# Hybrid attention block on one core: attention written as three merged streams in a fixed TensorE order

## The chip, the cores and the metric

The kernel runs on one core of one Trainium2 chip. The time is the device time of one execution in microseconds (us). The core has five engines with instruction streams of their own: TensorE (PE in the profile, PEld for its weight loads), VectorE (DVE), ScalarE (ACT), GpSimd (POOL) and SyncE (SP), which here does nothing but issue DMA transfers. Each engine runs its own instructions in their order, and waits where an operand or a buffer isn't ready.

## The reference

One decoder block on x of shape (1, 1024, 1024) in float32:

```python
h = rms_norm(x, g_pre)
qa, ka, va, fa, za, qb, kb, vb, zb, gates = split(h @ w_in)
# branch a: 8 "fox" heads of 64, causal softmax attention with a forget term
logits = q @ k.T / 8 + c[:, None] - c[None, :]      # c = cumsum(log_sigmoid(fa + b_forget))
ya = softmax(causal(logits)) @ v * silu(za)
# branch b: 4 "diff" heads; q and k are pairs of 64, with rope
yb = (softmax(q1 @ k1.T) - lam * softmax(q2 @ k2.T)) @ v
yb = rms_norm(yb, g_subln) * (1 - lam_init) * silu(zb)
merged = sigmoid(gate_a) * (ya @ w_branch[0]) + sigmoid(gate_b) * (yb @ w_branch[1])
out = x + rms_norm(merged @ w_out, g_post)
```

## The kernel before

**Stages.** x is normalised and transposed into hT, and the v parts of the projection are computed and spilled to DRAM (0 to 111 us). Then come eight attention units (111 to 605): unit u = 0 to 3 is diff head u, unit 4 to 7 is a pair of fox heads. Then the gate projections g0 to g7 (605 to 775), in which each pair after g0 is computed by a Winograd-like scheme of seven products x1 to x7 of 12 matmuls (`gates_pair`, `wino`), the branch products pb (781 to 871) and the output (871 to 967).

**Precision.** Every product is made of three matmuls in a split format: an operand is cut into hi (a cast) and lo (the rest), and hi·hi, hi·lo and lo·hi are summed in PSUM. So a weight tile comes as a DMA into `raw_*`, a cast `hi_*` (POOL) and a subtraction `lo_*` (DVE); the probabilities P as a transposed tile `pt`, a cast `ph` (ACT) and a subtraction `pl` (DVE); and q and k as stacked tiles TA, TB (q) and KA, KB (k), which hold hi in one half of the partitions and lo in the other, with X0 and X1 as copies of TA and TB with the halves swapped, made by DMA (`swapped`). A logits piece `S` is two matmuls, one with TA and one with X0 (TB and X1 for the second map).

**A projection** (q, k or z of one unit) is two chunks of 512 columns, each 8 k-steps of 3 matmuls: `pk`, `pq`, `pz`. A q or k chunk is copied to `rawq`, `rawk` by ACT. For diff units its halves are swapped by four DMAs into `swq`, `swk`, multiplied by sines (POOL L292) and cosines (DVE L291), added (L293), and stacked (ACT L298 and L300, DVE L299 and L301). A z chunk goes to DRAM.

**A unit** has the groups g = 0 to 3 of two 128-row blocks (fox: for each of two heads). `row` computes the logits of one block in pieces of up to 512 columns into three PSUM buffers (`Sd`, `Sf`), from which DVE adds the bias and keeps the running extreme (L442, tile `mxd` or `mxf`); ACT takes the exponential (L446). In a diff unit POOL then combines the two maps (L534, L536). `av` transposes P (`ptd`, `ptf`), splits it, and multiplies with V (`ypd`, `ypf`). The order in the code is: the rows of a group, the products of the group behind (`pend`), then some tasks of a list `fill`, which holds the next unit's q and k chunks and z projections in whole chunks:

```python
tasks = [mk("k", 0, ...), mk("q", 0, ...), mk("k", 1, ...), mk("q", 1, ...)]
```

A scheduler with a time model of its own then sets the order of each engine's instructions, so that matmuls of a chunk, logits and products come out interleaved. The lists `ZFILL`, `TFILL` and `SFILL` say in which unit z projections, operand sums for the gates (`h_combinations`) and sums of squares for the diff heads' norm (`sum_squares`, ssq) stand.

**The gates.** For pair d two weights are fetched (`raw{d}_0`, `raw{d}_1`, L829). POOL forms sums S1 to S4 and splits the operands a2 and a4 (L685); ACT casts all seven. Between the pairs stand `y_work(t, c)`, which multiply the finished attention outputs (`yd` for t = 0 to 3, diff; `yf` for t = 4 to 7, fox) with norm factors `rb` and silu(z) `zs`: DVE, POOL (L797), ACT (L798), DVE. `YORD[d]` lists those that stand behind pair d. The branches then need `yT`, casts of yf and yd by ACT (L864), and weights `hi_br`.

## Time and profile before

| | us |
|---|---|
| three runs | 968.75, 968.38, 965.19 |
| median | 968.38 |
| the profiled execution | 969.32 |
| its span | 967.2 |
| mean granted PE clock | 0.982 |

The span is the time from the first to the last instruction that the profile shows. Rows of the timeline give start and duration in us, engine, line, operation, out<-in by the program's names without their numbers, and in brackets the idle time of that engine just before and what ended it. Matmuls are pipelined: one of 512 columns is shown with some 0.39 us, and the next starts 0.23 us after it. SPq rows are DMA issues; their duration is that of the issue, not of the transfer.

### The profile page before, as it was taken

What the parts mean: (1) busy time and instruction counts of PE and PEld (TensorE: products, weight loads), DVE (VectorE), ACT (ScalarE), POOL (GpSimd) and SP (SyncE); (2) the same over time, 40 slices, a digit from 0 to 9 for tenths busy, and PEclk for the clock granted to TensorE, in tenths of its full rate; (3) what the DMA queues carried; (4) which work ended last, traced back from release to release, by engine and by line L of the source; (5) the groups of instructions that cost most, each with busy time, mean ns of one, the idle gap of its engine ahead of it and who ended that gap; (6) DMA issues with size and microseconds to landing.
All of it is one profiled execution on the core that took longest, in us unless ns stands there. A gap on an engine that the chain in (4) does not pass through costs nothing. (4 is left out here: it accounts for less than half of the span.)

```text
span 967.2 us, 13623 instructions
## 1 busy us (share of the span) xinstructions
PE 902.9 (93%) x4608; PEld 752.5 (78%) x4608; DVE 614.8 (64%) x1100; ACT 416.0 (43%) x838; POOL 443.3 (46%) x401
## 2 busy tenths in 40 slices
PE   7999989999998999999999998999999879999993
PEld 5999867788777878878878887777887658887872
DVE  6731258878677657586585676147565683549866
ACT  3421124555555565475664767224333361313431
POOL 7100035546555364251331442236555636787964
PEclk9999989999999999999999999999999989999997
DMA  8532444425234353353443432984545696211232
GB/s 312 190 109 96 143 127 119 111 63 147 83 110 121 90 150 129 109 173 100 125 159 104 116 120 90 377 327 130 159 150 157 205 361 211 85 47 44 88 130 87
DMA packets 120710, 139.10 MB, mean 144 GB/s; under 512 B 11473, under 2 KB 85297, under 8 KB 119618
## 3 DMA queue, kind: packets, MB, share of 16 engines
q1 hardware_dynamic: 120642, 138.24, 44.8%
q8 instruction: 36, 0.59, 0.3%
q14 instruction: 32, 0.26, 0.1%
HBM read 87.76 MB, written 37.86 MB: 130 GB/s over the span
## 5 line engine op out<-in xcount | busy, mean ns | idle before, releaser
L198 PE MATMUL pv<-wvhi,hT 128*128 128x264 f32 (+2 forms) x384 | 89.0, 324 | 0.4 <-DVE hT L184 0.4
L733 PE MATMUL x_g<-T,a_g 128*128 128x512 f32 x336 | 80.9, 397 | 6.3 <-ACT a_g L684 5.5
L249 PE MATMUL pk<-hT,hi_k 128*128 128x512 f32 x256 | 85.1, 405 | 1.5 <-ACT rawk L286 1.5
L559 POOL TENSOR_TENSOR cb<-cb,trim 128x128 f32<-128x128 f32 x64 | 35.2, 552 | 111.3 <-DVE mxf L442 99.2
L875 PE MATMUL pb<-yT,hi_br 128*128 128x512 f32 x256 | 80.3, 397 | 5.8 <-ACT hi_br L235 5.8
L249 PE MATMUL pz<-hT,hi_z 128*128 128x512 f32 x256 | 83.6, 396 | 0.0
L249 PE MATMUL pq<-hT,hi_q 128*128 128x512 f32 x256 | 83.1, 396 | 0.0
L733 PE MATMUL x_o<-wo_op,a_o 128*128 128x512 f32 x336 | 77.9, 391 | 3.8 <-POOL a_o L685 2.5
L733 PEld LDWEIGHTS x_g<-T,a_g 128*128 128x128 f32 x336 | 63.8, 191 | 21.8 <-ACT a_g L684 6.8
L733 PEld LDWEIGHTS x_o<-wo_op,a_o 128*128 128x128 f32 x336 | 62.7, 188 | 18.8 <-POOL a_o L685 3.8
L446 ACT ACTIVATE Pd<-Pd,mxd 128x1024 f32<-128x1024 f32 (+7 forms) x64 | 49.7, 777 | 59.1 <-DVE mxd L442 58.7
L198 PEld LDWEIGHTS pv<-wvhi,hT 128*128 128x128 f32 x384 | 64.5, 190 | 6.1 <-DVE hT L184 0.7
L733 PE MATMUL x_g<-hT,a_g 128*128 128x512 f32 x252 | 61.4, 398 | 2.8 <-DVE a_g L685 2.8
L446 ACT ACTIVATE Pf<-Pf,mxf 128x768 f32<-128x768 f32 (+4 forms) x64 | 49.8, 778 | 29.3 <-DVE mxf L442 28.9
L198 PE MATMUL pv<-wvlo,hT 128*128 128x512 f32 (+2 forms) x192 | 61.8, 324 | 0.4 <-DVE wvlo L154 0.4
L471 DVE TENSOR_TENSOR plf<-ptf,phf 128x512 fp32r<-128x512 f32 (+1 forms) x80 | 50.1, 635 | 18.7 <-ACT phf L470 17.5
L875 PEld LDWEIGHTS pb<-yT,hi_br 128*128 128x128 f32 x256 | 49.1, 192 | 16.5 <-ACT hi_br L235 6.2
L733 PEld LDWEIGHTS x_g<-hT,a_g 128*128 128x128 f32 x252 | 48.3, 192 | 13.8 <-DVE a_g L685 3.7
L534 POOL TENSOR_SCALAR Pd<-Pd,l 128x128 f32<-128x128 f32 (+7 forms) x32 | 28.5, 893 | 65.7 <-DVE l L532 51.4
L249 PEld LDWEIGHTS pk<-hT,hi_k 128*128 128x128 f32 x256 | 48.1, 193 | 10.6 <-issue 1.9
L442 DVE CUSTOM_DVE_ANT_0 Pf<-Sf,cb 128x512 f32<-128x512 f32 (+1 forms) x64 | 36.1, 569 | 29.6 <-PE Sf L441 16.3
L249 PEld LDWEIGHTS pz<-hT,hi_z 128*128 128x128 f32 x256 | 47.4, 188 | 8.6
(250 smaller groups left out, 2352.8 us busy)
## 6 DMA issues: line engine op xcount, KB each, us to landing
t_d<-t SPq DMA_DIRECT2D x32, 256.0 KB, 2.5
T<-t_d SPq DMA_DIRECT2D x8, 1024.0 KB, 7.7
raw<-in_w_in_dram SPq DMA_DIRECT2D x14, 512.0 KB, 6.3
g_d<-c_g SPq DMA_DIRECT2D x21, 256.0 KB, 2.4
vb_d<-vbs SPq DMA_DIRECT2D x8, 512.0 KB
va_d<-vas SPq DMA_DIRECT2D x8, 512.0 KB, 3.6
raw_k<-in_w_in_dram SPq DMA_DIRECT2D x8, 512.0 KB, 5.3
raw_q<-in_w_in_dram SPq DMA_DIRECT2D x8, 512.0 KB, 4.0
```

The source lines that it names most:

```text
L198: nc.tensor.matmul(ps[n], lhsT=hT[hp][k // 4][i // 4][:, k % 4, hs], rhs=wt[k][:, a:b], start=first, stop=(k == KT - 1 and hp == 1))
L249: nc.tensor.matmul(ps, lhsT=a[:, k, :], rhs=hT[h][k // 4][c][:, k % 4, :], start=(k == 0 and a is hi and h == 0), stop=(k == KT - 1 and a ...
L442: nc.vector.tensor_tensor_reduce(out=pr[:, a:b], in0=ps, in1=bias[:, boff + a:boff + b], scale=-0.125, scalar=BIG if j == 0 else mx[:, j - ...
L446: nc.scalar.activation(pr[:, 0:n], pr[:, 0:n], AF.Exp, bias=mx[:, len(pcs) - 1:len(pcs)], scale=-1.0, accum_out=le)
L471: nc.vector.tensor_tensor(pl[:, 0:n], pt[:, 0:n], ph[:, 0:n], op=ALU.subtract)
L534: nc.gpsimd.tensor_scalar(p2[:, 0:n], p2[:, 0:n], l2, 1.0, op0=ALU.mult, op1=ALU.mult)
L559: nc.gpsimd.tensor_tensor(diag, diag, trim, op=ALU.add)
L733: nc.tensor.matmul(x[m], lhsT=a[:, ai, k, :], rhs=right[m][bi][k], start=(k == 0 and n == 0), stop=(k == 3 and n == 2))
L875: nc.tensor.matmul(ps, lhsT=a[:, kk, :], rhs=yT[g][h][:, k % 2, sl], start=(k == 0 and a is hi and h == 0), stop=(k == 3 and a is lo))
```

## The change

**Attention.** Each unit's work becomes lists of steps with an estimated PE time: a k-step of a projection (3 matmuls), one piece of logits (2 matmuls), the transposes or the products of one tile. For each group `merge` sorts three such streams by the fraction of the group's time at which they shall stand: its share of the next unit's projections over the whole group, its own logits over the first 0.75 (the unit's first group 0.3 to 0.85), and the products of the group behind from 0.25 on. For PE alone, and for attention alone, the order of the code is kept (`manual_schedule`); the other engines' orders are still set by the scheduler. A class `Jobs` runs the projections one after the other, k chunk 0, k chunk 1, q chunk 0, q chunk 1, then z, and fetches the weight of the next one at the second k-step of the current one. The X copies are made one group ahead, the loads of V and of the fox bias a unit ahead, the logarithms of the forget term in unit 0, and squares ahead of their sums. z2 moves from unit 3 to unit 2, z3 from 4 to 3, z4 from 5 to 4, so that unit 5 has none; `h_combinations(0)` moves from unit 4 to 3.

**Gates.** `YORD` puts the fox outputs first, in twos and threes, and the loads of yf come first.

```diff
-TFILL = ((), (), (), (), (0,), (1,), (2,), (3,))
+TFILL = ((), (), (), (0,), (), (1,), (2,), (3,))
...
-YORD = ((), ((0, 0),), ((0, 1), (1, 0)), ((1, 1), (2, 0)), ((2, 1), (4, 0), (4, 1)),
-        ((3, 0), (5, 0), (5, 1)), ((3, 1), (6, 0), (6, 1), (7, 0), (7, 1)), ())
-ZFILL = ((0,), (1,), (), (2,), (3,), (4,), (5,), (6, 7))
+YORD = ((), ((4, 0), (4, 1)), ((5, 0), (5, 1), (6, 0)), ((6, 1), (7, 0), (7, 1)),
+        ((0, 0), (0, 1), (1, 0)), ((1, 1), (2, 0), (2, 1)), ((3, 0), (3, 1)), ())
+ZFILL = ((0,), (1,), (2,), (3,), (4,), (), (5,), (6, 7))
...
+        st.enter_context(tc.manual_schedule(engines={mybir.EngineType.PE}))
...
+            jobs = [(f"{kind}{u}", c0 + t * P, [chunk(kind, c) for c in range(2)])
+                    for kind, c0 in (("k", kc), ("q", qc))]
...
+            def steps(self, count):
+                todo = []
+                for n in range(self.at, self.at + count):
+                    nm, _, outs = self.jobs[n]
+                    for c in range(2):
+                        box = {}
+                        for k in range(KT):
+                            def run(n=n, nm=nm, c=c, k=k, box=box, out=outs[c]):
+                                if k == 0:
+                                    self.fetch(n)
+                                    box[0] = pj.tile([P, CH], F32, tag="pj", name=f"p{nm}_{c}")
+                                if k == 1 and c == 0:
+                                    self.fetch(n + 1)
+                                hi, lo = self.w[n]
+                                for a, h in ((hi, 0), (hi, 1), (lo, 0)):
+                                    nc.tensor.matmul(...)
+                                if k == KT - 1:
+                                    out(box[0])
+                            todo.append((0.68, run))
+                self.at += count
+                return todo
...
+            return [(2 * ((b - a) / 2400 + 0.014), lambda j=j, a=a, b=b: step(j, a, b))
+                    for j, (a, b) in enumerate(pcs)]
...
                 if jj <= g:
-                    trans(jj)
+                    steps.append((0.44, lambda jj=jj: trans(jj)))
                 if jj >= SKEW:
-                    prod(jj - SKEW)
-            evac(yp)
+                    steps.append((0.48 if fox else 0.72, lambda jj=jj: prod(jj - SKEW)))
+            steps.append((0.0, lambda: evac(parts["y"])))
...
+        def merge(*streams):
+            order = []
+            for a, b, steps in streams:
+                total = sum(w for w, _ in steps) or 1.0
+                at = 0.0
+                for wt, fn in steps:
+                    order.append((a + (b - a) * (at + 0.5 * wt) / total, len(order), fn))
+                    at += wt
+            for _, _, fn in sorted(order, key=lambda o: o[:2]):
+                fn()
...
+            for n, (prep, rows, prd) in enumerate(groups):
+                done += sized[n]
+                part = []
+                while fill and (n == len(groups) - 1 or fdone < total * done / sum(sized)):
+                    part.append(fill.pop(0))
+                    fdone += part[-1][0]
+                ahead = []
+                if n + 1 < len(groups):
+                    ahead.append(fixed(groups[n + 1][0]))
+                if n == 1 and u < 7:
+                    ahead.append(fixed(units[u + 1][0], 0))
+                merge((0.0, 0.0, ahead), (0.0, 1.0, part),
+                      (0.3 if n == 0 else 0.0, 0.85 if n == 0 else 0.75, rows()),
+                      (0.25, 1.0, prods))
+                prods = prd
...
-    for t in range(4):
+    for t in (4, 5, 6, 7, 0, 1, 2, 3):
         y_load(t)
```

**The start of unit 0.** In the order's rows a name carries its unit or tile first (rawq0_0 is unit 0, chunk 0) and a buffer number last. ACT at the first q and k chunks, before:

```order
L286 COPY rawk0_0_1211<-pk0_0_1186 128x512
L598 ACTIVATE le_1168<-le_1168 128x2
L286 COPY rawq0_0_1256<-pq0_0_1231 128x512
L298 CAST KA0_1178<-rawk0_0_1211 64x512
L300 CAST KB0_1179<-rawk0_0_1211 64x512
L286 COPY rawk0_1_1295<-pk0_1_1270 128x512
L298 CAST TA0_1176<-rawq0_0_1256 64x512
L300 CAST TB0_1177<-rawq0_0_1256 64x512
L286 COPY rawq0_1_1334<-pq0_1_1309 128x512
```

and now:

```order
L287 COPY rawk0_0_1255<-pk0_0_1224 128x512
L638 ACTIVATE le_1170<-le_1170 128x2
L287 COPY rawk0_1_1294<-pk0_1_1269 128x512
L299 CAST KA0_1180<-rawk0_0_1255 64x512
L301 CAST KB0_1181<-rawk0_0_1255 64x512
L287 COPY rawq0_0_1339<-pq0_0_1308 128x512
L299 CAST KA0_1180<-rawk0_1_1294 64x512
L301 CAST KB0_1181<-rawk0_1_1294 64x512
L287 COPY rawq0_1_1378<-pq0_1_1353 128x512
```

The copy of q chunk 0 stood ahead of the KA and KB casts of chunk 0, and stands behind them now; the copy of k chunk 1 is ahead of them. On PE the first logits stand among k chunk 0 of the next unit, pk1_0. Before:

```order
L249 MATMUL pk1_0_1404<-hT000_90,hi_k1_1400 128x512
L440 MATMUL Sd0_0_0_0_1363<-KA0_1178,TA0_1176 128x128
L249 MATMUL pk1_0_1404<-hT100_94,hi_k1_1400 128x512
L249 MATMUL pk1_0_1404<-hT000_90,lo_k1_1401 128x512
L440 MATMUL Sd0_1_0_0_1370<-KB0_1179,TB0_1177 128x128
L440 MATMUL Sd0_0_1_0_1382<-KA0_1178,TA0_1176 128x256
L249 MATMUL pk1_0_1404<-hT010_92,hi_k1_1400 128x512
L249 MATMUL pk1_0_1404<-hT110_96,hi_k1_1400 128x512
L249 MATMUL pk1_0_1404<-hT010_92,lo_k1_1401 128x512
L249 MATMUL pk1_0_1404<-hT010_92,hi_k1_1400 128x512
L249 MATMUL pk1_0_1404<-hT110_96,hi_k1_1400 128x512
L441 MATMUL Sd0_0_0_0_1363<-KA0_1178,X0d0_0_1354 128x128
```

and now:

```order
L353 MATMUL pk1_0_1407<-hT000_90,hi_k1_1314 128x512
L353 MATMUL pk1_0_1407<-hT100_94,hi_k1_1314 128x512
L353 MATMUL pk1_0_1407<-hT000_90,lo_k1_1315 128x512
L468 MATMUL Sd0_0_0_0_1422<-KA0_1180,TA0_1178 128x128
L469 MATMUL Sd0_0_0_0_1422<-KA0_1180,X0d0_0_1393 128x128
L468 MATMUL Sd0_1_0_0_1429<-KB0_1181,TB0_1179 128x128
L469 MATMUL Sd0_1_0_0_1429<-KB0_1181,X1d0_0_1396 128x128
L353 MATMUL pk1_0_1407<-hT000_90,hi_k1_1314 128x512
L353 MATMUL pk1_0_1407<-hT100_94,hi_k1_1314 128x512
L353 MATMUL pk1_0_1407<-hT000_90,lo_k1_1315 128x512
```

Before, 10 matmuls of pk1_0 stood ahead of the first logits, and 7 more between their first half (with TA) and the second (with X0d); now 6 stand ahead, and the halves follow one another.

**Inside a diff unit.** PE in unit 2, at row block 6 (Sd2_map_block_piece); the first rows from before, the second from now:

```order
L491 MATMUL ypd2_1_2819<-phd2_1_0_2821,V2_2534 128x256 x2
L491 MATMUL ypd2_1_2819<-pld2_1_0_2822,V2_2534 128x256
L440 MATMUL Sd2_0_6_0_2906<-KA2_1927,TA2_1925 128x512
L441 MATMUL Sd2_0_6_0_2906<-KA2_1927,X0d2_3_2897 128x512
L440 MATMUL Sd2_0_6_1_2910<-KA2_1927,TA2_1925 128x384
L441 MATMUL Sd2_0_6_1_2910<-KA2_1927,X0d2_3_2897 128x384
L440 MATMUL Sd2_1_6_0_2917<-KB2_1928,TB2_1926 128x512
L491 MATMUL ypd2_1_2819<-phd2_1_1_2830,V2_2534 128x256 x2
L441 MATMUL Sd2_1_6_0_2917<-KB2_1928,X1d2_3_2900 128x512
L491 MATMUL ypd2_1_2819<-pld2_1_1_2831,V2_2534 128x256
```

```order
L353 MATMUL pq3_1_2954<-hT011_93,lo_q3_2600 128x512
L468 MATMUL Sd2_0_6_0_2995<-KA2_1188,TA2_1186 128x512
L469 MATMUL Sd2_0_6_0_2995<-KA2_1188,X0d2_3_2819 128x512
L353 MATMUL pq3_1_2954<-hT011_93,hi_q3_2599 128x512
L353 MATMUL pq3_1_2954<-hT111_97,hi_q3_2599 128x512
L353 MATMUL pq3_1_2954<-hT011_93,lo_q3_2600 128x512
L353 MATMUL pq3_1_2954<-hT011_93,hi_q3_2599 128x512
L353 MATMUL pq3_1_2954<-hT111_97,hi_q3_2599 128x512
L353 MATMUL pq3_1_2954<-hT011_93,lo_q3_2600 128x512
L468 MATMUL Sd2_0_6_1_3019<-KA2_1188,TA2_1186 128x384
L469 MATMUL Sd2_0_6_1_3019<-KA2_1188,X0d2_3_2819 128x384
```

Before, three pieces of logits follow one another directly; now six matmuls of a projection stand between two pieces.

**The gates.** POOL in pair g3, where a4 is the last reader of raw3_1 (L797, now L895, is the product of a y_work). Before:

```order
L697 TENSOR_TENSOR S4_g3_7234<-raw3_0_7130,S2_g3_7154 128x512
L797 TENSOR_TENSOR yd0_6812<-yd0_6812,zs0_1_7114 128x512
L685 TENSOR_TENSOR a2_g3_7215<-raw3_0_7130,a2_g3_7215 128x512
L797 TENSOR_TENSOR yd0_6812<-yd0_6812,zs1_0_7122 128x512
L685 TENSOR_TENSOR a4_g3_7255<-raw3_1_7132,a4_g3_7255 128x512
L697 TENSOR_TENSOR S1_g4_7318<-raw4_1_7298 128x512
```

and now:

```order
L795 TENSOR_TENSOR S4_g3_7264<-raw3_0_7160,S2_g3_7184 128x512
L895 TENSOR_TENSOR yf2_6815<-yf2_6815,zs5_0_7133 128x512
L783 TENSOR_TENSOR a2_g3_7245<-raw3_0_7160,a2_g3_7245 128x512
L895 TENSOR_TENSOR yf2_6815<-yf2_6815,zs5_1_7142 128x512
L895 TENSOR_TENSOR yf3_6818<-yf3_6818,zs6_0_7151 128x512
L783 TENSOR_TENSOR a4_g3_7285<-raw3_1_7162,a4_g3_7285 128x512
L795 TENSOR_TENSOR S1_g4_7353<-raw4_1_7333 128x512
```

One y_work stood between the splits of a2 and a4, and the pair had two; now two stand there, and the pair has three. ACT at the end of the gates, before:

```order
L684 CAST a3_g7_7949<-S4_g7_7947 128x512
L798 ACTIVATE zs6_1_7797<-zs6_1_7797 128x512
L798 ACTIVATE zs7_0_7806<-zs7_0_7806 128x512
L798 ACTIVATE zs7_1_7815<-zs7_1_7815 128x512
L864 CAST yT0_2_7973<-yf2_7290 128x1024 x2
L864 CAST yT0_3_7979<-yf3_7293 128x1024 x2
L235 CAST hi_br0_0_8000<-raw_br0_0_7997 128x1024
```

and now:

```order
L896 ACTIVATE zs3_1_7819<-zs3_1_7819 128x512
L782 CAST a2_g7_7931<-raw7_0_7827 128x512
L900 ACTIVATE cu2_g6_7709<-cu2_g6_7709 128x512
L782 CAST a3_g7_7952<-S4_g7_7950 128x512
L959 CAST yT0_2_7976<-yf2_6815 128x1024 x2
L959 CAST yT0_3_7982<-yf3_6818 128x1024 x2
L235 CAST hi_br0_0_8003<-raw_br0_0_8000 128x1024
```

The sigmoids zs of the last three y_works stood between the a3 cast of g7 and the casts yT; they are gone from there.

## The prediction

> **What bounds the kernel now.** I read the page's totals first, then the busy time by stage, then what TensorE (PE) waits for, then single stretches of the timeline. The totals say which engine sets the time:

> ```profile
> span 967.2 us, 13623 instructions
> PE 902.9 (93%) x4608; PEld 752.5 (78%) x4608; DVE 614.8 (64%) x1100; ACT 416.0 (43%) x838; POOL 443.3 (46%) x401
> ```

> PE is busy 93% of the span; no other engine passes 64%. The change leaves PE's matmuls the same in number and shape, so time can only come from PE's idle stretches and its half-clock stretches, or go into new ones. By stage (stretch, length, busy time of PE, PEld, DVE, ACT, POOL, granted PE clock, DMA share, GB/s):

> ```profile
> 111.00:149.00 38.00, 33.80 (x137) 26.93 (x137) 20.41 (x33) 8.64 (x20) 8.65 (x7) 0.91 0.50 137
> 149.00:317.00 168.00, 158.19 (x832) 131.40 (x831) 132.67 (x304) 89.29 (x195) 90.12 (x78) 0.99 0.39 105
> 317.00:606.00 289.00, 279.06 (x1596) 236.62 (x1595) 193.76 (x443) 168.55 (x364) 108.48 (x122) 1.00 0.40 123
> 606.00:785.00 179.00, 163.91 (x692) 132.12 (x691) 99.56 (x115) 66.97 (x110) 85.87 (x59) 0.96 0.67 225
> ...
> 649.40:652.80 3.40, 3.40 (x10) 2.61 (x8) 2.97 (x2) 0.00 (x0) 3.40 (x3) 0.50 0.12 45
> 779.10:785.90 6.80, 4.51 (x10) 3.09 (x11) 6.80 (x7) 6.80 (x9) 3.06 (x1) 0.50 1.04 388
> ```

> The rows are the start of attention, diff units 0 to 2 (with the first logits of 3), the rest of unit 3 with fox units 4 to 7, and the gates with the start of the branches. Idle: 4.2, 9.8, 9.9 and 15.1 us. The last two rows are stretches at half clock, each 3.4 us or two of that: matmuls then take double, so a stretch costs about 1.7 us. What the idle time waits for, over the whole run (total, times, longest):

> ```profile
> PE pb L875 <- ACT hi_br L235: 5.8, 1, 5.8
> PE x_g L733 <- ACT a_g L684: 5.5, 3, 3.5
> PE Sd L440 <- DVE mxd L442: 5.2, 7, 1.4
> PE x_g L733 <- DVE a_g L685: 3.6, 4, 1.8
> PE Sf L440 <- DVE mxf L442: 3.2, 5, 1.3
> PE ptd L467 <- POOL Pd L536: 2.3, 1, 2.3
> PE ptf L467 <- DVE plf L471: 2.0, 5, 1.0
> PE ssq L359 <- POOL sq L356: 1.6, 1, 1.6
> ```

> Sd and Sf wait because logits stand in clusters and only three PSUM buffers hold them until DVE has read them; no single wait dominates.

> **The change, term by term.** All against the profiled execution, 969.3 us (span 967.2 and 2.1 around it). It lies 0.9 above the median of the three runs, 968.4.

> *Start of unit 0 (loss).* Before, the order is k chunk 0, q chunk 0, k chunk 1, q chunk 1; now both k chunks come first, so q chunk 0 leaves PE 5.4 us later, and on ACT its copy now stands behind the KA and KB casts. Those, and what follows:

> ```profile
> 133.36 0.62 ACT L298 CAST KA<-rawk 64x512 fp32r<-64x512 f32 x1 [9.78 <-DVE rawk L293]
> 134.00 0.62 ACT L300 CAST KB<-rawk 64x512 fp32r<-64x512 f32 x1
> ...
> 135.25 2.41 SPq L290 DMA_DIRECT2D swk<-rawk  x4
> 139.28 1.36 POOL L292 TENSOR_TENSOR swk<-swk,sinT 128x512 f32<-128x512 f32 x1 [5.05 <-DMA swk<-rawk]
> 142.56 1.21 DVE L239 TENSOR_TENSOR lo_q<-raw_q,hi_q 128x1024 fp32r<-128x1024 f32 x1
> 144.52 0.69 DVE L301 TENSOR_TENSOR KB<-rawk,KB 64x512 fp32r<-64x512 f32 x1
> 143.83 1.23 SPq L413 DMA_DIRECT2D X0d<-TA  x2
> X0d<-TA SPq DMA_DIRECT2D x32, 64.0 KB, 2.8
> 146.79 0.62 PE L249 MATMUL pq<-hT,hi_q 128*128 128x512 f32 x2
> ```

> The casts end at 134.6, and the copy that stood third there was k chunk 1; now it is q chunk 0, so q takes the place in the pipeline that k chunk 1 had: swap issued 135.25, rotated by POOL until 140.6, the DVE work behind lo_q, TA and TB complete by about 144 to 145. Then X0d and X1d are cut from them (1.2 us of SP each, 2.8 us to landing): the first logits can finish at about 147 and 148. Before, TA was ready some 5 us sooner and the first halves of the logits stood ahead of the X halves with matmuls of pk1_0 between. Now only 6 matmuls of pk1_0 stand ahead of Sd0_0_0 and both halves are adjacent, so PE stands from about 137 to 148. At 148.1 before had done the 18 other matmuls of pk1_0 (4.1 us, finished at 146.79), 1.3 us of pq1_0 and 0.3 us of logits: 5.7 us ahead. A stop of 11 us also brings one or two half-clock stretches, 1.7 to 3.4. Loss 8 us; ends 5 (the swaps land sooner) and 11. raw_z0's fetch now stands on SP ahead of swq0_0, but SP is idle there until the copy; no cost. The first V loads keep their place.

> *Diff units (gain).* The stream spaces logits about a k-step (three matmuls) apart, so the Sd waits (5.2) should go; the forget logarithms a unit earlier and z2 as filler in unit 2, which had none, take smaller ones. h_combinations(0), work of DVE, ACT and POOL, moves into unit 3, where from 317 to 345 PE waited for nothing; if that cover goes, Sd waits return there, within the lower end. PE idles 9.8 there, plus one half-clock stretch (0.99 of 168 us, 1.7), plus about 0.2 per wait that the modelled ends hide (15 waits, 3): 14. What comes back: at each unit boundary ptd_3_0 needs the chain of row 7:

> ```profile
> L442 DVE CUSTOM_DVE_ANT_0 Pd<-Sd,dmask,mxd 128x512 f32<-128x512 f32 x6 | 4.5, 747 | 0.1
> L446 ACT ACTIVATE Pd<-Pd,mxd 128x1024 f32<-128x1024 f32 x6 | 6.9, 1152 | 4.2 <-DVE mxd L442 4.1
> L534 POOL TENSOR_SCALAR Pd<-Pd,l 128x1024 f32<-128x1024 f32 x3 | 3.4, 1125 | 4.0 <-DVE l L532 2.0 <-DVE fs L611 2.0
> L536 POOL TENSOR_TENSOR Pd<-Pd,Pd 128x1024 f32<-128x1024 f32 x3 | 7.2, 2388 | 0.1
> ```

> 0.75 + 1.15 + 1.13 + 2.39, and about 0.7 of accumulator reads and the two tiny DVE steps, is 6.1 us before any queueing; the fixed order puts 6.0 us of PE work between the last Sd of row 7 and ptd_3_0. I give each of three boundaries two waits of 0.8: 5. Gain 9; ends 0 (every wait comes back elsewhere) and 14. Loads moved earlier (weights one projection ahead, V, cum_d rows) cost nothing while the DMA share is 0.39 to 0.40; if that cover goes, a 0.5 MB weight would come too late for its first k-step.

> *Fox units (about even).* Waits on Sf (3.2) and ssq (1.6, the squares now a quarter unit ahead) go. But between the last transpose into a ptf and the first product that uses it, a chain must fit:

> ```profile
> L470 ACT CAST phf<-ptf 128x512 fp32r<-128x512 f32 x48 | 27.5, 583 | 11.9 <-PE ptf L467 10.9
> L471 DVE TENSOR_TENSOR plf<-ptf,phf 128x512 fp32r<-128x512 f32 x48 | 32.6, 689 | 17.0 <-ACT phf L470 16.3
> ```

> 1.27 us with no queue. Adding up PE's work between the two for all 80 tiles, at 227 ns per 512 columns, the median falls from 4.4 to 1.8 us; the shortfalls below 1.3 add up to 4.6 us before and 8.5 now. Before, 2.0 shows as ptf waits, so the growth is 1.7 (in that proportion) to 3.9; I take 3. Unit 5 loses its z (48 matmuls, 10.9 us) and waits about 1 us more at its end. Gain 4.8 less 4: 1. Ends: gain 6 (none of the waits return), loss 11 (third paragraph of the rivals).

> *Gates (loss).* POOL runs the third y_work of a pair ahead of the a4 split, the last reader of that pair's second weight; only then is the next one fetched. The four second fetches, the wait that follows, and 24 matmuls:

> ```profile
> 678.60 0.38 SPq L829 DMA_DIRECT2D raw<-in_w_in_dram  x1
> 698.92 0.38 SPq L829 DMA_DIRECT2D raw<-in_w_in_dram  x1
> 723.88 0.38 SPq L829 DMA_DIRECT2D raw<-in_w_in_dram  x1
> 747.40 0.38 SPq L829 DMA_DIRECT2D raw<-in_w_in_dram  x1
> 753.75 0.73 PE L733 MATMUL x_g<-T,a_g 128*128 128x512 f32 x2 [3.48 <-ACT a_g L684]
> 769.78 5.60 PE L733 MATMUL x_g<-hT,a_g 128*128 128x512 f32 x24
> ```

> A pair is 84 matmuls of 227 ns, 19.1 us. With two y_works (the first interval) the fetches come 20.3 apart; with three, 25.0 and 23.5, some 5 us behind PE per pair. Before, that happens twice: the first uses up the slack, the second costs the 3.48. Now YORD has three at d=2 to 5, four times: two more at about 3.5 each, 7. Ends: 0 (t = 0 to 3 take one rb fetch instead of two, so their y_works end sooner), and 15 (four intervals of 24.3 against 19.1 make 20.8, less the 5.3 of before).

> [...] In this trace a 1.8 us wait (x_g on DVE) stands right ahead of the half-clock stretch at 649.4, so I would count 1.7 for each of the two new stops, which 7 does not hold and the upper end does. [...]

> *Branch start (gain).* pb0 waits for hi_br, behind the last y_works:

> ```profile
> 765.64 0.60 ACT L684 CAST a_g<-S_g 128x512 fp32r<-128x512 f32 x1
> ...
> 776.31 3.87 ACT L864 CAST yT<-yf 128x1024 fp32r<-128x1024 f32 x4
> 780.08 1.04 ACT L235 CAST hi_br<-raw_br 128x1024 fp32r<-128x1024 f32 x1
> ```

> The four casts wait for the last yf products, which were t = 6 and 7 at d=6 and are now done at d=3. ACT is then free for casts and hi_br (4.9 us together) straight after the a3 cast of g7 (the first row), while PE works on pair 7 until 775.4, 9.1 us longer. Gain 5.8 and the half-clock stretches of 779.1 to 785.9 (3.4): 9.2. Ends 5 (half of it late with a3) and 9.2.

> Sum: +8 − 9 − 1 + 7 − 9.2 = −4.2, so 965.1 against the profiled 969.3 and, by the same shift, 964 against the median.

> **The rivals.** *Even spacing works better than I grant it:* the attention waits go entirely (14 and 6 instead of 9 and 1) and the swaps of unit 0 land early (5 instead of 8): 964 − 13, or 951. For it: of 19.7 us idle in 149 to 606, 12.3 are the waits of Sd, Sf, ptd and ssq listed above. Against it: the fixed order can't slip another matmul in front when something is late.

> *Slower, by the products of the fox units:* DVE is in order, and a logits reduction or another plf (0.69 us each) often stands ahead of the plf that PE now needs. With 0.9 us of queue the chain is 2.2 us; the shortfalls of 80 tiles then add to 43.5 now and 27.1 before, 16 more, of which I count 11, and half-clock stretches come with them; 964 + 12 + 2 is 978. It decides once the mean chain passes about 2.1 us. For it: median room of 1.8 us. Against it: DVE is busy only 194 of 289 us there, and before showed 2.0 where 4.6 was possible.

> *The gates' lag becomes steady:* 15 instead of 7, with everything else as forecast: 972, no measurable change.

> **How the numbers follow.** Forecast (sum near −4) 0.45, own range 957 to 972; better spacing 0.2; fox products 0.2; steady lag 0.15. This kernel's runs lie within 0.4% of each other, so 0.5% (below 963.5, above 973.2) is what can be told from no change. Faster: half of the forecast case, 0.22, nearly all of the second, 0.19, and 0.03 of the others: 0.44. Slower: 0.14 of the fox case, 0.05 of the lag and 0.03 of the forecast: 0.22. Same: 0.34. The range reaches from 948 (better spacing with the gates at 3) to 980.

> **What would show it.** Start: PE idle around 137 to 148 with X0d or X1d as releaser; wrong if the first Sd comes before 145. Diff: no Sd waits on mxd beyond 1 us in total, ptd waits on Pd at three boundaries. Fox: ptf and ypf waits on plf of 5 to 10 us in total, above 15 the slower rival. Gates: waits on a_g in g5 to g7, 16 us in all against 9.1. Branches: the wait on hi_br below 1 us. The forecast is wrong if the first logits don't stall, if hi_br still waits, or if PE's fixed order meets transfers that I took for hidden.

## The result and the profile after

The changed kernel takes 1010.2 us (median of four runs, 1009.6 to 1013.4), against 968.1 before (the three runs above and a fourth): slower by 4.5%, ratio 1.045 with a 95% interval of 1.0426 to 1.0474. The forecast was 964 and the range ended at 980. The page's totals, span and busy time of each engine:

```profile
span 1007.6 us, 13646 instructions
PE 914.3 (91%) x4608; PEld 758.7 (75%) x4608; DVE 616.3 (61%) x1100; ACT 422.4 (42%) x838; POOL 447.6 (44%) x401
```

The work is the same and PE waits more. To see where, I took the times from one matmul's start to the next, subtracted the best spacing of each shape (227 ns at 512 columns, 117 at 256, 108 for a transpose) and summed the rest as PE's loss per stage, half-clock time included. The first row holds the start and all of unit 0, and the gates' row ends at the first pb, so that the wait on hi_br counts there:

| stage, up to | before | after | change |
|---|---|---|---|
| start and unit 0 (first logits of unit 1) | 12.1 | 25.5 | +13.4 |
| units 1 to 3 (first logits of unit 4) | 17.5 | 23.6 | +6.1 |
| fox units 4 to 7 (first gate matmul) | 27.4 | 56.6 | +29.2 |
| gates (first pb) | 20.5 | 14.6 | −5.9 |
| branches and output | 7.4 | 4.8 | −2.6 |

The sum is +40.2; the spans differ by 40.4. So attention lost 48.7 us, and the gates and what follows gained 8.5. Of what PE waits for now, over the whole run, the rows that bear on the change (total, times, longest):

```profile
PE ypf L524 <- DVE plf L503: 19.5, 25, 2.5
PE Sd L468 <- DVE TA L300: 7.4, 1, 7.4
PE ptd L499 <- POOL Pd L571: 6.7, 4, 2.5
PE Sd L468 <- DVE mxd L470: 6.5, 3, 3.0
PE x_g L831 <- ACT a_g L782: 6.0, 4, 2.7
PE ypd L524 <- DVE pld L503: 4.4, 3, 2.5
PE ypf L524 <- ACT phf L502: 2.6, 8, 1.0
PE x_g L831 <- DVE a_g L783: 2.0, 4, 0.9
```

The first row is new in size: the products of the fox units wait for the low part of the transposed probabilities. Before, such waits were 0.6 us on the products, as this row shows, and 2.0 on the transposes:

```profile
PE ypf L491 <- DVE plf L471: 0.6, 3, 0.2
```

The wait of pb on hi_br (5.8) is gone. One of the 25 waits of the first row, in unit 6; first DVE, then PE:

```profile
558.38 0.69 DVE L503 TENSOR_TENSOR plf<-ptf,phf 128x512 fp32r<-128x512 f32 x1
558.98 0.97 DVE L419 SCALAR_TENSOR_TENSOR sub_rs<-sub_l,sub_rs 128x8 f32<-128x8 f32 x1
559.87 0.68 DVE L406 TENSOR_TENSOR f<-f,f 128x512 f32<-128x512 f32 x1
560.47 0.68 DVE L408 TENSOR_TENSOR f<-f,f 128x512 f32<-128x512 f32 x1
561.08 0.47 DVE L470 CUSTOM_DVE_ANT_0 Pf<-Sf,cb,mxf 128x256 f32<-128x256 f32 x1
...
561.59 0.68 DVE L300 TENSOR_TENSOR TA<-pq,TA 64x512 fp32r<-64x512 f32 x1
562.30 1.23 DVE L239 TENSOR_TENSOR lo_z<-raw_z,hi_z 128x1024 fp32r<-128x1024 f32 x1
563.45 0.55 DVE L503 TENSOR_TENSOR plf<-ptf,phf 128x384 fp32r<-128x384 f32 x1
```

```profile
561.31 0.28 PE L524 MATMUL ypf<-phf,V 128*128 128x256 f32 x1
564.05 0.39 PE L524 MATMUL ypf<-plf,V 128*128 128x256 f32 x1 [2.47 <-DVE plf L503]
564.45 0.79 PE L353 MATMUL pz<-hT,hi_z 128*128 128x512 f32 x2
```

DVE is never idle here: six other operations stand between two plf. PE issues the product with phf at 561.31 and then stands until the plf of 563.45 is done, though the k-steps of z that come next (564.45) need nothing that DVE still has to make.

### The profile page after: what moved, and what is told of

Read it like the earlier page. It is cut to its first block, busy times and chain, and to the rows that moved or that the text cites. A ratio compares the mean times of both kernels' runs of the same rounds, so it can differ in the third digit from the quotient of the medians.

```text
span 1007.6 us, 13646 instructions
## 1 busy us (share of the span) xinstructions
PE 914.3 (91%) x4608; PEld 758.7 (75%) x4608; DVE 616.3 (61%) x1100; ACT 422.4 (42%) x838; POOL 447.6 (44%) x401
## 5 line engine op out<-in xcount | busy, mean ns | idle before, releaser
L598 POOL TENSOR_TENSOR cb<-cb,trim 128x128 f32<-128x128 f32 x64 | 30.1, 473 | 165.5 <-DVE mxf L470 143.5
L475 ACT ACTIVATE Pd<-Pd,mxd 128x128 f32<-128x128 f32 (+7 forms) x64 | 49.7, 777 | 53.8 <-DVE mxd L470 53.0
L470 DVE CUSTOM_DVE_ANT_0 Pf<-Sf,cb 128x512 f32<-128x512 f32 (+1 forms) x64 | 36.7, 574 | 44.2 <-PE Sf L469 39.0
L524 PE MATMUL ypf<-plf,V 128*128 128x256 f32 (+1 forms) x160 | 44.2, 309 | 19.7 <-DVE plf L503 19.5
L475 ACT ACTIVATE Pf<-Pf,mxf 128x1024 f32<-128x1024 f32 (+3 forms) x64 | 49.8, 778 | 28.2 <-DVE mxf L470 27.7
L502 ACT CAST phf<-ptf 128x512 fp32r<-128x512 f32 (+1 forms) x80 | 42.6, 542 | 34.0 <-PE ptf L499 30.8
```

The source lines that it names most:

```text
L470: nc.vector.tensor_tensor_reduce(out=pr[:, a:b], in0=ps, in1=bias[:, boff + a:boff + b], scale=-0.125, scalar=BIG if j == 0 else mx[:, j - ...
L475: nc.scalar.activation(pr[:, 0:n], pr[:, 0:n], AF.Exp, bias=mx[:, j:j + 1], scale=-1.0, accum_out=le)
L502: nc.scalar.copy(ph[:, 0:n], pt[:, 0:n])
L524: nc.tensor.matmul(o, lhsT=a, rhs=b[:, src], start=(j == 0 and n == 0), stop=(odd == 1 and jj == g and n == len(prods) - 1))
L598: nc.gpsimd.tensor_tensor(diag, diag, trim, op=ALU.add)
```

## The experiments

Times are medians of each run; the kernel before, run beside them, took 966.6 to 968.1 us. Two words for what follows: the room of a tile is PE's own work between its last transpose and its first product, and its chain is the time from the end of that transpose through the cast on ACT to the end of the subtraction on DVE. The theory after the result: the fixed order leaves less room than the chain takes (theory A). The rival: the other parts, job order and shifted lists, cost (theory B).

**Without the fixed order.**

```diff
-        st.enter_context(tc.manual_schedule(engines={mybir.EngineType.PE}))
```

> The changed kernel with the fixed TensorE order in attention given up: the same steps, jobs and tables, but the scheduler orders PE again. Theory A (the fixed order leaves too little PE work between a tile's transposes and its products, and DVE's queue is longer than that): the room between the two, summed over PE's order, is 4.65 us in the median again (1.83 with the fixed order, 4.40 before), so the 29 us lost in the fox units and most of the 6 lost in diff units 1 to 3 go: 962 to 977 us, ypf waits on plf below 3 us in total instead of 19.5. Theory B (the order of the jobs k0 k1 q0 q1 and the shifted z and h_combinations lists are what costs): they are all still there, so 995 us or more.

Measured: 956.0 us, ratio to before 0.988 (0.985 to 0.991). Its largest waits in attention:

```profile
PE Sd L467 <- DVE mxd L469: 5.5, 6, 1.7
PE ptf L498 <- DVE plf L502: 2.7, 5, 0.7
PE Sd L467 <- DVE TA L299: 2.4, 1, 2.4
PE ypf L523 <- ACT phf L501: 2.2, 2, 2.0
```

The products' waits on plf are gone from the list, and the time is not only back but 11 us below the kernel before. So that one line costs 54 us, and all else in the change together gains. Theory B falls as the main cause. The other engines' orders change with that line, too, but DVE doesn't become quicker by it: a tile's chain in the fox units is longer here, 2.55 us on average against 2.00 in the changed kernel. What is larger is the room, 4.65 us in the median against 1.83, and the waits went with the room.

**Where the fixed order costs.** The line applied to some units only:

```diff
+        hold = ExitStack()
+        hold.enter_context(tc.manual_schedule(engines={mybir.EngineType.PE}))   # units 0 to 3
...
+            if u == 4:
+                hold.close()
```

> The changed kernel with PE's order fixed in units 0 to 3 (diff) only; the scheduler orders PE from unit 4 on. By PE's loss beyond the matmuls' own time, the changed kernel loses 13.4 us more than before in the start and unit 0, 6.0 in units 1 to 3 and 29.0 in the fox units. If the loss sits where it shows: 1010 less what the fox units lost, so 975 to 982 us. If the fixed order's loss were one thing that a later stage takes over (a delay handed on), most of it would stay: above 990 us.

Measured: 974.0 us, just below the first range.

> The changed kernel with PE's order fixed in units 4 to 7 (fox) only. The room between transposes and products in the fox units is 1.83 us in the median, as in the changed kernel, and that of the diff units is the scheduler's. If the loss sits where it shows: e1's 956 and the fox units' 29 to 33, so 984 to 990 us, with ypf waits on plf of 17 to 21 us. If the fox waits come from an order that the diff units hand over: 960 to 975 us.

Here the stack is entered at u == 4 and closed behind the last products. Measured: 997.3 us, with this wait in front:

```profile
PE ypf L523 <- DVE plf L502: 19.3, 23, 2.5
```

Against e1 the diff units with the start cost 18.0 us (e10 loses 47.8 up to unit 4, nearly as the changed kernel with 49.1, and 22.0 in the fox units instead of 56.6), and the fox units 41.4, more than the 28 to 34 expected. Together 59 for the 54 of both: the two parts are nearly independent, and the fox waits need no diff units in front of them.

**More room by a longer skew.** The skew is the number of tiles by which the products stand behind the transposes.

```diff
-SKEW = 1
+SKEW = 2
```

> The changed kernel with SKEW 2 instead of 1: the products of a tile stand two tiles of transposes behind instead of one, PE order still fixed. Theory A: the room between transposes and products in the fox units rises from 1.83 to 2.53 us in the median, and the shortfalls below 1.9 us fall from 28.5 to 17.2 (18.0 before): ypf waits on plf fall from 19.5 to about 10, time 990 to 998 us. Theory B: no room matters, 1007 to 1013 us.

Measured: 1020.6 us, 10 slower instead of 12 to 20 faster. Its waits on the subtractions:

```profile
PE ptf L499 <- DVE plf L503: 12.0, 10, 3.1
PE ptd L499 <- DVE pld L503: 10.6, 7, 3.5
PE ypf L524 <- DVE plf L503: 6.8, 10, 1.5
```

The wait of the products fell from 19.5 to 6.8, so room does what theory A says of it. But the wait came back one step earlier: the transposes of the next tile wait for one of two PSUM buffers that the same late subtraction still reads. With a third buffer for them, taken from the logits:

```diff
-SKEW = 1
+SKEW = 2
...
-        sps = ... name="sps", bufs=3, ...
-        tps = ... name="tps2", bufs=2, ...
+        sps = ... name="sps", bufs=2, ...
+        tps = ... name="tps2", bufs=3, ...
```

> [...] In e2 the waits on plf and pld did not go: they moved from the products (ypf 6.8) to the transposes (ptf 12.0, ptd 10.6), which waited for a buffer that the late subtraction still read. If it is room in both places that lacks: ptf and ptd waits on pl fall below 8 us together, ypf stays about 7, and unless two logits buffers cost as much, 995 to 1003 us. If DVE is simply too slow for this order: the waits move on to Sd and Sf, 1010 to 1025 us.

Measured: 1012.5 us, in the second range.

```profile
PE Sd L468 <- DVE mxd L470: 15.7, 11, 3.7
PE ypf L524 <- DVE plf L503: 12.8, 16, 2.3
```

The waits of the transposes on the subtractions are gone from the list. Those of the products came back in part, from 6.8 in e2 to 12.8, and the fox units lose 45.0 us instead of 56.6. The diff units give it back: Sd waits 15.7 us instead of 6.5, and units 1 to 3 lose 32.5 instead of 23.6. Two logits buffers instead of three would do that, and so would a DVE that is too slow for this order, as the second expectation has it; no run tells the two apart.

**Room by another share of filler.** Filler is here the next unit's projections, which PE can do while a chain runs. Each group's share of the projections goes by the products beside it:

```diff
-            for prep, rows, prd in groups:
+            for prd in [prods] + [g[2] for g in groups[:-1]]:
                 sized.append(sum(wt for wt, _ in prd))
```

> The changed kernel, PE order fixed, with each group's share of the projections measured by the products that run beside it (those of the group behind) instead of by its own. In the fox units, where groups shrink from 4 tiles to 1, the changed kernel gives a large group's products the small fill of the next: in its trace 15.9 of the 22.2 us of waits of fox products fall on the 23 of 80 tiles with less than 1.3 us of PE work behind their transposes. Here 14 tiles have less (14 before, too), and the shortfalls below 1.9 us add up to 18.9 instead of 28.5 us. If the lack of room is the cause: ypf waits on plf fall from 19.5 to 10 to 13 us and the time to 992 to 1000 us. If the wait is handed to another place as in the two SKEW runs: 1005 to 1013 us.

Measured: 1014.5 us, just above the second range.

```profile
PE ypf L524 <- DVE plf L503: 13.1, 19, 2.1
PE Sd L468 <- DVE TA L300: 13.1, 1, 13.1
PE ptd L499 <- POOL Pd L571: 11.1, 6, 4.1
...
PE ptf L499 <- ACT Pf L475: 5.0, 4, 2.6
```

The wait on plf fell as far as expected, and the time rose: unit 0's first group has no products behind it and now gets no filler (13.1 on TA), and the transposes wait longer for Pd and Pf (11.1 and 5.0, against 6.7 and 1.1). The fox units lose 52.7 instead of 56.6. The filler was moved, not made.

**A shorter queue on DVE.**

```diff
-                    self.w[n] = load_w(self.jobs[n][0], w_cols(self.jobs[n][1]))
+                    self.w[n] = load_w(self.jobs[n][0], w_cols(self.jobs[n][1]), False, True)
```

> The changed kernel with the low parts of the 24 attention weights (L239) subtracted by POOL instead of DVE; PE's order is the same instruction for instruction. If the late plf is a matter of DVE's queue (blocks of 1.2 us of low-part subtractions, h_combinations and casts stand ahead of it): 24 blocks of 1.23 us leave DVE, ypf and ypd waits on pl fall from 23.9 to about 15, time 998 to 1004 us. If it is only the length of the chain (cast 0.58 and subtraction 0.69, with DVE free): no change, 1008 to 1012 us. If POOL becomes late for Pd instead: ptd waits on Pd rise above 10 us.

Measured: 1017.9 us, outside both ranges; the third outcome, a late POOL, came.

```profile
PE ypf L524 <- DVE plf L503: 20.9, 26, 2.8
PE ptd L499 <- POOL Pd L571: 13.4, 6, 4.4
```

The plf waits didn't fall. Summed over the 80 fox tiles, the time from the end of a phf cast to the start of its plf is 46.1 us in the changed kernel and 43.7 here; the weights' low parts (L239) fill only 4.5 of the 46.1, the logits reductions 10.8, the operand sums of h_combinations (L398 to L411) 11.3. I had taken the longest operation for the largest share. POOL, with 24 more operations, became late for Pd.

**DVE in the code's order, too.**

```diff
-        st.enter_context(tc.manual_schedule(engines={mybir.EngineType.PE}))
+        st.enter_context(tc.manual_schedule(engines={mybir.EngineType.PE, mybir.EngineType.DVE}))
```

> The changed kernel with DVE kept in the order of the code too, inside attention, beside PE. Where the scheduler put f12, f11 and lo_z6 ahead of plf6_0_2_2, the code's order has only the logits reductions and the casts of q there. If the loss comes of two engines ordered by different rules (PE by hand, DVE by a model that thinks PE elsewhere): plf waits fall from 19.5 to 5 to 10 us, time 985 to 1000 us. If the queue on DVE is as long in any order, because DVE's own work per tile is what it is: 1005 to 1015 us. If DVE, held in code order, stops for rope inputs that come by DMA: slower, above 1015 us, with DVE idle behind swk or swq.

Measured: 1122.6 us. Three rows of what PE waits for, and two of what DVE waits for:

```profile
PE Sd L468 <- DVE mxd L470: 46.4, 10, 9.1
PE ypf L524 <- DVE ys L611: 29.7, 3, 11.8
PE ypf L524 <- DVE plf L503: 12.7, 21, 2.6
```

```profile
DVE rawk L292 <- DMA swk<-rawk: 40.8, 8, 11.1
DVE rawq L292 <- DMA swq<-rawq: 20.5, 5, 7.2
```

The third outcome: DVE stops for the rope operands, 61.3 us in 13 waits, and with it everything that needs DVE. A second engine held in hand order makes the whole worse. Whether part of the loss comes of ordering PE and DVE by different rules isn't settled: the wait on plf fell from 19.5 to 12.7, while the stops of DVE hid what else the order did.

**The start alone.** Unit 0's four chunks as before, PE's order still fixed (in `Jobs.steps`):

```diff
+                if self.at == 0:
+                    todo_order = [(n, c) for c in range(2) for n in range(count)]
```

> The changed kernel with unit 0's own projections in the order k chunk 0, q chunk 0, k chunk 1, q chunk 1, as before; all else, and PE's fixed order behind it, as changed. The start (110.8 to the first logits of unit 1) loses 25.5 us beyond the matmuls' own time, and 12.1 in the kernel before. If the order of the four chunks is the cause, TA and X0 come some 5 us sooner and the waits Sd on TA (7.4) and on X0d (2.1) go: 1000 to 1003 us. If it is that only 6 matmuls of pk1_0 stand ahead of the first logits and the two halves are adjacent: the wait stays in part, 1004 to 1008 us.

Measured: 1006.5 us, in the second range. The first logits come at 138.8 instead of 145.5 us, but the waits at the units' ends rise:

```profile
PE ptd L502 <- POOL Pd L574: 11.6, 8, 3.7
```

**The gates alone.** The kernel before with the new `YORD` and the loads of yf first.

> The kernel before with only the gates' part of the change: the new YORD and the loads of yf first; attention as before. If the stages add up, the gates and the branch start give what the two traces show between them (loss above the matmuls' own time 22.7 before, 14.5 after, so 8 us): 958 to 962 us. If that gain hangs on the changed attention (fox outputs done earlier or other leftovers): 965 to 969 us. The forecast of the prediction for these two terms was a gain of 2 us, so 966.

Measured: 963.5 us, ratio 0.997 (0.995 to 0.999). Between the two expectations: a gain of 3.4 us in the medians; in its trace the stretch from the first gate matmul to the first pb is 3.9 us shorter than before, and the rest 2.8 shorter. In the changed kernel these were 5.3 and 2.5. So the gates' part gives 3.4 of the 11 us that the version without the fixed order gains.

**Versions without the fixed order.** The start's chunk order, the old lists, and both:

> The version without the fixed order (e1, 956.0 us, 11 below the kernel before) with unit 0's projections in the order k chunk 0, q chunk 0, k chunk 1, q chunk 1. e1 still waits 2.4 us for TA and 1.7 for rawq at the start, and its first logits come at 144.9 against 141.7 before. If the chunk order costs with any PE order: 951 to 954 us. If the scheduler already covers it: 955 to 957 us.

Measured: 954.7 us, ratio 0.986 (0.983 to 0.988), between the two ranges.

> The version without the fixed order (e1, 956.0 us) with the lists ZFILL and TFILL of the kernel before, so that z2 stands in unit 3, z3 in 4, z4 in 5 and h_combinations(0) in unit 4 again. e1 is 11 us faster than before, of which the gates' part alone gives 3.4 (e4). If the moved lists bring the rest (unit 2 with filler; before it lost 8.4 us beyond the matmuls' time, the most of the first seven units): 960 to 965 us. If it is the steps, the job order and the earlier loads: 954 to 958 us.

The edit puts back the two lists `TFILL` and `ZFILL` shown with the change. Measured: 953.2 us, ratio 0.986 (0.984 to 0.989), the fastest. So the moved lists are not what gains. Beside the gates' 3.4 us it is the steps, the order of the jobs or the earlier loads, which no run separates.

> No fixed order, unit 0's chunks in the order k q k q (as in e9, 954.7 us) and the lists ZFILL and TFILL of before (as in e12, 953.2 us), both at once. If both gains (1.3 and 2.8 us against e1's 956.0) are real and add up: 950 to 953 us. If they are noise of the scheduler's choice: 953 to 957 us. Either way faster than both kernels.

Measured: 959.8 us, ratio 0.992 (0.991 to 0.994), outside both ranges. The two small edits don't add up: each edit lets the scheduler choose another order for PE, and its waits on mxd went from 7.9 us in e12 to 12.6 here. Differences of a few us between such versions say little about the edit that was meant.

## Why the prediction was wrong, point by point

**Start (+8 forecast, +10 measured): the mechanism held, the size was a little short.** The table's +13.4 also holds unit 0's attention, which the forecast put among the diff units. Up to the end of the half-clock stretch at 155.2 PE had lost 18.1 us, and 8.0 up to 149 before, so the start lost 10.1 more, inside the ends of 5 and 11. The rows of PE:

```profile
135.22 1.19 PE L353 MATMUL pk<-hT,hi_k 128*128 128x512 f32 x2 [2.45 <-ACT rawq L287]
...
145.51 0.45 PE L468 MATMUL Sd<-KA,TA 128*128 128x128 f32 x1 [7.39 <-DVE TA L300]
148.09 0.44 PE L469 MATMUL Sd<-KA,X0d 128*128 128x128 f32 x1 [2.13 <-DMA X0d<-TA]
149.42 0.45 PE L469 MATMUL Sd<-KB,X1d 128*128 128x128 f32 x1 [0.67 <-DMA X1d<-TB]
```

TA by 144 to 145, X0d at 147 and X1d at 148 were forecast; the matmuls that use them started within 1.5 us of that. What was missing is the clock: I allowed one or two half-clock stretches of 3.4 us, and up to 155.2 half clock covers 17.1 us, against 6.8 before. The longest stretch, in a row like those of the prediction's stages:

```profile
141.60:155.20 13.60, 6.89 (x19) 5.63 (x20) 9.52 (x20) 4.65 (x12) 2.83 (x5) 0.50 0.27 67
```

**Diff units (−9 forecast, +9.4 measured: 3.3 in unit 0's attention, 6.1 in units 1 to 3): the step that failed is "the Sd waits should go".** 6.5 us of them stayed, in three waits of up to 3.0, where before seven made 5.2. The boundaries, put at 5 in all, took 6.7 on Pd and 4.4 on pld. The two long Sd waits, of 2.97 us up to 187.93 and of 2.77 up to 231.72, stand behind other work of DVE, that of the forget term and of the next unit's q and k. The second begins while DVE makes the cumulative sum, and the stacking of KA, 1.58 us, follows before DVE reads the logits:

```profile
226.77 2.69 DVE L674 TENSOR_TENSOR_SCAN cum<-ones,lf 8x1024 f32<-8x1024 f32 x1
...
231.72 0.38 PE L468 MATMUL Sd<-KB,TB 128*128 128x256 f32 x1 [2.77 <-DVE mxd L470]
```

The forecast had counted the earlier logarithms of the forget term as a small gain. Spaced logits don't help when DVE is late for other reasons, since in the fixed order nothing else may pass the one that waits.

**Fox units (−1 forecast, +29.2 measured): this is the step that made the forecast wrong.** The waits of their products on plf and phf grew from 0.8 to 22.1 us, and half clock from 0 to 14 us of these units, worth up to 7. The term came from the right row and the right sum (room 1.83 us in the median, chain 1.27 without a queue), but I scaled the growth of the shortfalls by the 2.0 us of ptf waits that the kernel before showed, and took 3. That scale was the error. The queue was already there: from the last transpose to the finished plf a tile took 2.23 us on average before, and 2.00 after; with 1.9 to 2.2 us instead of 1.3 as the chain, the shortfalls were 18 to 27 us before and 28 to 44 now. That alone is a growth of 10 to 16, less than came. The rest is that a shortfall cost little in the old order and much in the new one. A likely reason, which no run isolates, is that the scheduler's order had 43 of the 80 tiles with over 4 us of room; the changed order has none, and 23 tiles with under 1.3 us, on which 15.9 of its 22.2 us of product waits fall. Long chains add to it: the 25 tiles that waited for plf had a room of 1.15 us and a chain of 2.10 in the median, the other 55 had 2.06 and 1.62.

The second rival had this mechanism and the row for it (room of 1.8), at 978 and a chance of 0.2. Its deciding point, a mean chain past 2.1 us, was not reached (2.00), and its price was too low: 11 us more of shortfalls where the waits grew by 21, and 2 for half clock where up to 7 came.

**Gates (+7 forecast, about 0 measured).** The second fetches of the pairs now:

```profile
730.58 0.38 SPq L927 DMA_DIRECT2D raw<-in_w_in_dram  x1
752.62 0.38 SPq L927 DMA_DIRECT2D raw<-in_w_in_dram  x1
774.81 0.38 SPq L927 DMA_DIRECT2D raw<-in_w_in_dram  x1
798.02 0.38 SPq L927 DMA_DIRECT2D raw<-in_w_in_dram  x1
```

They come 22.0, 22.2 and 23.2 us apart, not 24.3, so the slack lasts longer than I reckoned; that this alone spared the waits isn't shown. Waits on a_g are 8.0 us against 9.1 before, and the seven products take 146.6 us against 147.4. The row order that I saw was right; the period was taken from only two intervals of the old mix.

**Branch start (−9.2 forecast, −8.4 measured): right.**

```profile
821.11 1.05 ACT L235 CAST hi_br<-raw_br 128x1024 fp32r<-128x1024 f32 x1
824.10 1.07 PE L970 MATMUL pb<-yT,hi_br 128*128 128x512 f32 x4
```

hi_br is ready at 822.2, 1.9 us before PE needs it. The first branch matmul starts 0.2 us after the last x_g matmul started, instead of 6.2, and the 2.4 us that half clock cost behind them are gone: 8.4.

**The sum.** Between the profiled executions (965.1 forecast, 1009.6 measured) it missed by 44 us: 30 in the fox term, 18 in the diff term and 2 at the start, with 6 back from the gates and the branch start. Against the medians (964 and 1010.2) it is 46. The two large ones are of one kind: I priced a fixed order by the waits that the free order had shown, when the free order had been made to avoid them. "The fixed order can't slip another matmul in front when something is late" stood in the prediction as an argument against one rival, not as a cost.

**What stays open.** That the fixed order costs 54 us is shown, and that its largest wait is short room ahead of late subtractions; how the 54 us divide between waits, half clock and the rest is my accounting from the traces. Each run that gave more room cut those waits (to 6.8, 12.8 and 13.1 us), yet none got the time back: buffers, ends of units or the start took over. No run found a fixed order as good as the scheduler's, so whether one exists isn't shown.

## What to carry to other kernels

A hand-written order for an engine must be judged by the distance between each producer step and its consumer, in that engine's own work, against the time from one to the other that the trace shows with its queues (here 2.0 to 2.2 us, not the 1.27 of the operations). Waits that a tuned order shows say little about what another order will wait for: price the new order by the old trace's latencies, not by its waits alone. Even that would have fallen short here, by 10 to 16 us against 21. And when a change bundles an order with other edits, run it without the order first: here the rest was worth 11 us.

## What the hardware showed that I had not expected

Waits of 1.9 and 2.5 us of PE were followed by half clock, that up to 454.73 from 455.6 to 459.0, and that up to 564.05 by

```profile
564.90:568.30 3.40, 3.40 (x11) 2.61 (x11) 2.81 (x6) 1.16 (x3) 1.01 (x2) 0.50 0.86 213
```

In the kernel before, a wait of 1.83 us up to 649.05 was followed by half clock from 649.41 to 652.82. Half clock covers 37.8 us of attention after and 10.2 before. By my estimate, from 3.41 us at a granted clock of 0.50, such a short stop cost up to 1.7 us beside its own length. Not every such stop did: the 2.77 us up to 231.72 and the 2.51 up to 313.93 were followed by full clock.
